# A transformer block on one core: the turn from attention to the feed-forward layer is put in another order, and w_down is loaded one block per step

## The chip, the core and the metric

The kernel runs on one core of one Trainium2 chip. The metric is device time in microseconds (us) of that core. Engines are named as in the profile: PE is the tensor engine (PEld its weight loads), DVE the vector engine, ACT the scalar engine, POOL the GpSimd engine, SP the engine that issues every DMA of this kernel.

## The reference

One block on 1024 tokens of width 1024, in float32. The mixer's three branches (a convolution branch, a chunked mLSTM, and a differential attention with four heads) are joined and multiplied by `w_out`; then a residual with a layer norm, a feed-forward layer of width 4096 with a squared ReLU, and a second residual with a layer norm:

```python
mix = jnp.concatenate([y_conv, y_ml, y_da], axis=-1) @ w_out
x1  = layer_norm(ALPHA * x + mix, ln1_g, ln1_b)
h   = jnp.square(jax.nn.relu(x1 @ w_up))
out = layer_norm(ALPHA * x1 + h @ w_down, ln2_g, ln2_b)
```

## The kernel before, in words

**Precision.** Every float32 operand is split into a high and a low part (`split`: ACT casts to `hi` at L147, DVE subtracts to `lo` at L148), and each product is three matmuls: hi by hi, lo by hi, hi by lo.

**Order of the work.** Instructions carry a priority and a scheduler lists them by it when the program is built: `lane(k)` gives the priority k million, and a lower number goes first when both could go. What stands on an engine is then a fixed row, which the engine works off in order. SP is such a row too: a DMA that waits there holds up all DMAs behind it. Buffers are 47 slots of 128 x 1056 in four rings (X, W, T, G), joined to one ring F for the feed-forward part; a buffer's load waits on SP until the slot's last user is done.

**Out projection** (`out_proj`, L854): y (the joined branches, kept in DRAM as `ydram0` to `ydram7`) times `w_out`, in two calls. The first takes y's blocks 0 to 4, the second blocks 5 to 7 (the attention's), for eight rows of 128 tokens each: 18 matmuls of 128x512 per row, which DVE adds to `acc` (L895), then a norm per row (`stats` on DVE, L903 on ACT). A row of y is read back by three DMAs (`yraw`), cast (`yh`) and subtracted (`yl`). The attention's last head (`attention(3, ...)`, lane 2) stands between the calls: scores `s`, softmax (`pp`), transposes into `t`, `wth`/`wtl`, their product with the values into `t`, a square sum (`sqs`), and `yda`, which goes out to `ydram` in four stores of 256 tokens.

**The turn.** `x1_half(t4)` transposes four rows of `acc` on PE (32 transposes) into two tiles of `xr`; half 0 gives B11 and B21, half 1 gives B12 and B22.

**The feed-forward layer** is a Strassen-Winograd product: seven products P1, P2, P6, P5, P7, P3, P4 in that order instead of eight. P1 needs B11 of x1, P2 needs B21, P6 needs T2, P5 needs T1, P7 needs T3, P3 needs B22, P4 needs T4, where T1 = B12 - B11, T2 = B22 - T1, T3 = B22 - B12, T4 = B21 - T2 (`x1_combine`). P1 and P2 of a pair thus need the first token half alone. w_up is worked off in 16 pairs of blocks; `up(s, p)` is one product of pair s, 12 matmuls of 128x512, and after P4 `hidden(s)` squares and stores the pair's hidden blocks (`h`). w_down follows in 56 steps of 24 matmuls (two halves of the output, seven products, four blocks each); step n needs its hidden operand (`hraw`, read from `h`), and its block or a sum of blocks of w_down (B11, B21, T2, ...), all split; `down_prep` issues that three steps ahead. Before, all of w_down's B12, B22 and B21 of the first half are asked for at step 0, the rows of the residual (`acc_load`) right behind it.

## Time and profile before

| | |
|---|---|
| median of 3 runs | 1198.04 us (1197.0 to 1199.02) |
| profiled execution | 1196.94 us, span 1195.2 us |
| mean granted PE clock | 0.984 |
| busy PE, DVE, ACT | 1139.2, 840.5, 563.2 us |
| DMA | 179.86 MB, mean 150 GB/s |

Times in the rows below are us from the start of the span of this one execution. The 1.74 us between the span and its time lie outside the rows. A row of a timeline is one instruction or several merged (x32): start, duration, engine, line, operation, what it writes and reads, and in brackets how long the engine stood idle just before it and which instruction released it.

### The profile page before, as it was taken

Reading aid. Unit: us, or ns where it says so; the run is one execution under the profiler, and the core shown is the slowest. Engines: PE = TensorE matmul, PEld = TensorE weight load, DVE = VectorE, ACT = ScalarE, POOL = GpSimd, SP = SyncE. Lnnn points to the kernel's source line nnn. Section 1 sums busy time; section 2 is a strip of 40 time slices with the busy share of each in tenths; the row PEclk is TensorE's granted clock in tenths of the full one; section 3 lists DMA queues with packets and bytes.
Section 4 is the critical chain, followed back from the end, with each engine's and each line's share of the span. In section 5 each row is a group of like instructions: output and inputs, shape, how many; then the busy total and the mean of one; then the engine's idle time right before and its main releaser. Section 6 shows DMA issues by size and latency. Waiting matters only on the chain.

```text
span 1195.2 us, 14972 instructions
## 1 busy us (share of the span) xinstructions
PE 1139.2 (95%) x5630; PEld 934.5 (78%) x5630; DVE 840.5 (70%) x1255; ACT 563.2 (47%) x910; POOL 13.8 (1%) x12
## 2 busy tenths in 40 slices
PE   8999999999999999976999999999989999999993
PEld 6898778877897877764888888888868888888882
DVE  5999568864774648869666777655778576766758
ACT  5212473575764627466544454444625332345411
POOL 0000000000000000000000000000000000000013
PEclk9999999999999999987999999999999999999997
DMA  7202144436635662421556465543984544353303
GB/s 276 70 10 71 37 130 132 149 128 182 167 107 191 198 187 64 156 98 53 184 179 245 167 229 194 178 162 119 321 312 158 194 162 161 107 169 124 106 27 114
DMA packets 82648, 179.86 MB, mean 150 GB/s; under 512 B 7760, under 2 KB 29328, under 8 KB 82576
## 3 DMA queue, kind: packets, MB, share of 16 engines
q1 hardware_dynamic: 82576, 178.91, 45.0%
q8 instruction: 44, 0.72, 0.2%
q14 instruction: 28, 0.23, 0.1%
HBM read 120.12 MB, written 58.72 MB: 150 GB/s over the span
## 4 chain that ended last, share of the span: by engine, by line
PE 84%; DVE 7%; ACT 4%; DMA 3%; issue 2%; SPq 0%; DVEq 0%; ACTq 0%
PE f L933 49%; PE mm L112 25%; PE s L112 5%; PE t L112 3%; PE t L115 2%; DVE lo L148 1%; ACT pp L736 1%; DMA hraw<-h 1%; DMA raw<-in_w_out 1%; ACT xr L975 1%; DVE bst L798 1%; ACT pp L741 1%; DMA kh<-qk 1%; DVE nm L734 1%; DVE pp L742 1%
## 5 line engine op out<-in xcount | busy, mean ns | idle before, releaser
L933 PE MATMUL f<-hi 128*128 128x512 f32 x832 | 330.6, 397 | 22.4 <-ACT hi L147 22.4
L933 PE MATMUL f<-lo,hi 128*128 128x512 f32 x832 | 329.6, 396 | 0.5 <-DVE lo L148 0.5
L933 PE MATMUL f<-hi,lo 128*128 128x512 f32 x832 | 328.4, 395 | 0.9 <-DVE lo L148 0.8
L933 PEld LDWEIGHTS f<-hi 128*128 128x128 f32 x832 | 158.2, 190 | 60.0 <-ACT hi L147 24.2
L933 PEld LDWEIGHTS f<-hi,lo 128*128 128x128 f32 x832 | 157.3, 189 | 38.8 <-DVE lo L148 2.8
L933 PEld LDWEIGHTS f<-lo,hi 128*128 128x128 f32 x832 | 158.2, 190 | 36.7 <-DVE lo L148 1.0
L147 ACT CAST hi<-hraw 128x1024 fp32r<-128x1024 f32 x56 | 58.1, 1048 | 104.7 <-DMA hraw<-h 93.2
L148 DVE TENSOR_TENSOR lo<-hraw,hi 128x1024 fp32r<-128x1024 f32 x56 | 68.3, 1222 | 51.1 <-ACT hi L147 48.5
L112 PE MATMUL mm<-xh,hi 128*128 128x512 f32 x240 | 95.8, 400 | 5.6 <-ACT xh L147 5.6
L112 PE MATMUL mm<-xl,hi 128*128 128x512 f32 x240 | 95.9, 400 | 0.0
L112 PE MATMUL mm<-xh,lo 128*128 128x512 f32 x240 | 95.9, 400 | 0.0
L285 DVE SCALAR_TENSOR_TENSOR cacc<-ypad,pc,cacc 128x1024 f32<-128x1024 f32 x60 | 74.2, 1278 | 0.6
L112 PE MATMUL mm<-hi,xh 128*128 128x256 f32 (+1 forms) x256 | 74.0, 289 | 0.0
L112 PE MATMUL mm<-hi,xl 128*128 128x256 f32 (+1 forms) x256 | 73.2, 286 | 0.0
L112 PE MATMUL mm<-lo,xh 128*128 128x256 f32 (+1 forms) x256 | 73.1, 286 | 0.0
L736 ACT ACTIVATE pp<-s,nm 128x128 f32<-128x128 f32 (+7 forms) x64 | 47.7, 747 | 28.7 <-DVE nm L734 19.7
L734 DVE TENSOR_REDUCE nm<-s 128x1 f32<-128x128 f32 (+7 forms) x64 | 47.9, 751 | 17.0 <-PE s L112 16.6
L147 ACT CAST hi<-B 128x1024 fp32r<-128x1024 f32 x32 | 33.5, 1050 | 50.6 <-PE f L933 34.5
L112 PEld LDWEIGHTS mm<-xh,hi 128*128 128x128 f32 x240 | 45.6, 190 | 14.3 <-ACT xh L147 5.6
L148 DVE TENSOR_TENSOR lo<-raw,hi 128x1024 fp32r<-128x1024 f32 (+3 forms) x34 | 39.2, 1160 | 24.2 <-ACT hi L147 19.8
L112 PE MATMUL mm<-hi,yh 128*128 128x512 f32 x128 | 50.9, 399 | 2.9 <-DVE tl L148 1.7
L112 PEld LDWEIGHTS mm<-xl,hi 128*128 128x128 f32 x240 | 45.6, 190 | 9.2 <-DVE xl L148 0.4
(258 smaller groups left out, 2039.1 us busy)
## 6 DMA issues: line engine op xcount, KB each, us to landing
hraw<-h SPq DMA_DIRECT2D x56, 512.0 KB, 3.5
w<-in_w_up SPq DMA_DIRECT2D x32, 512.0 KB, 3.9
B<-in_w_down SPq DMA_DIRECT2D x32, 512.0 KB, 5.9
h<-hp SPq DMA_DIRECT2D x16, 512.0 KB
h<-hq SPq DMA_DIRECT2D x16, 512.0 KB, 2.8
h<-hx SPq DMA_DIRECT2D x16, 512.0 KB, 4.4
raw<-in_wfm SPq DMA_DIRECT2D x14, 512.0 KB, 3.4
qk<-th SPq DMA_DIRECT2D x8, 512.0 KB
```

The lines of the kernel that those rows point to most:

```text
L112: return nc.tensor.matmul(out, lhsT=lhsT, rhs=rhs, start=start, stop=stop)
L115: nc.tensor.transpose(out, in_, ident[:k, :k])
L147: act.copy(hi, src)
L148: dve.tensor_tensor(out=lo, in0=src, in1=hi.bitcast(F32), op=ALU.subtract)
L285: dve.scalar_tensor_tensor(out=av, in0=yp[:, i:i + S], scalar=col(PC_DWW + 31 * c + i), in1=av, op0=ALU.mult, op1=ALU.add)
L734: dve.tensor_reduce(out=nm[:, m:m + 1], in_=s_[:, 0:nk], axis=AX.X, op=ALU.max, negate=True)
L736: act.activation(pp[m][:, 0:nk], s_[:, 0:nk], AF.Exp, bias=nm[:, m:m + 1], accum_out=sm[:, m:m + 1])
L741: act.activation(pp[1][:, 0:nk], pp[1][:, 0:nk], AF.Copy, scale=sm[:, 1:2])
L742: dve.scalar_tensor_tensor(out=pp[0][:, 0:nk], in0=pp[0][:, 0:nk], scalar=sm[:, 0:1], in1=pp[1][:, 0:nk], op0=ALU.mult, op1=ALU.add)
L798: dve.bn_stats(out=st[:, i, :], in_=z[:, i * (D // n):(i + 1) * (D // n)])
L933: return nc.tensor.matmul(out, lhsT=lhsT, rhs=rhs, start=start and not more, stop=stop and not more, skip_group_check=more)
L975: act.activation(xraw[kb // 4, t4][kb % 4 // 2][:, css[kb % 2]], t_, AF.Identity, scale=col(PC_L1G + kb), bias=col(PC_L1B + kb))
```

## The change

The attention's last head is emitted after a new lane 5, which holds the splits of `w_out`'s blocks 5 to 7 and the loads, sums and first splits of w_up's pairs 0 and 1. Rings X and W are joined to F before the last head, G after it, and the second `out_proj` takes all its buffers from F. `out_proj` calls `after_row` behind each row: it stores the row (`zdram`), loads pair 2 of w_up behind row 0, and behind row 5 emits `x1_half(0)` with its splits. `x1_half` now fills two banks at a time, and ACT and DVE evacuate one each. `x1_combine` is cut into five parts, and P1 and P2 of pairs 1 and 2 come before the first P6; then pairs 0 and 1 are worked off in turns. In the down part the blocks of w_down are loaded one or two per step, B11 and B21 from the last two up pairs on; the sums follow one per step, and for the first half T4 is written over B21.

```diff
-    def out_proj(kbs, first, rings, yring):
+    def out_proj(kbs, first, rings, yring, after=None):
...
                     act.activation(z, z, AF.Identity, scale=mv[:, 2:3], bias=mv[:, 4:5])
+                    after(tb)
         for r, w in zip(rings, wo):
             r.free(*w)
         early.clear()
 
     out_proj([0, 1, 2, 3, 4], True, [W] * NEARLY + [X] * (5 - NEARLY), lambda tb: X)
     X.give(W.take(2 * NEARLY))
-    with lane(2):
-        attention(3, neglam, dag)
-    out_proj([5, 6, 7], False, [X, G, G], lambda tb: X if tb > 1 else G)
-    psA.close()
-    ps_f = ctx.enter_context(tc.tile_pool(name="ps_f", bufs=1, space=bass.MemoryType.PSUM,
-                                          reuse_waits="tile"))
 
     F = Slots(spool, [])
-    for ring in (X, W, T, G):
+
+    def adopt(ring):
         F.q.extend(ring.q)
         F.of.update(ring.of)
+        ring.q.clear()
+
+    adopt(X)
+    adopt(W)
     zdram = [dram.tile([P, D], F32, name=f"z{i}") for i in range(TB)]
...
@@ -965,35 +965,52 @@
 
     xraw, xq = {}, {}
 
-    def x1_half(t4):
-        for kb in range(KB):
-            if kb % 4 == 0:
-                xraw[kb // 4, t4] = [F.alloc(F32, "xr") for _ in range(2)]
-            t_ = bank()
-            for j in range(4):
-                tr(t_[:, j * P:j * P + P], acc[4 * t4 + j][:, kb * P:kb * P + P])
-            act.activation(xraw[kb // 4, t4][kb % 4 // 2][:, css[kb % 2]], t_, AF.Identity,
-                           scale=col(PC_L1G + kb), bias=col(PC_L1B + kb))
+    def x1_half(t4, two_banks):
+
+        for i in range(2):
+            xraw[i, t4] = [F.alloc(F32, "xr") for _ in range(2)]
+        for kb in (0, 4, 2, 6):
+            t_ = two_banks()
+            for k in range(2):
+                for j in range(4):
+                    tr(t_[k][:, j * P:j * P + P],
+                       acc[4 * t4 + j][:, (kb + k) * P:(kb + k) * P + P])
+                o = xraw[kb // 4, t4][kb % 4 // 2][:, css[k]]
+                g_, b_ = col(PC_L1G + kb + k), col(PC_L1B + kb + k)
+                if k == 0:
+                    act.activation(o, t_[k], AF.Identity, scale=g_, bias=b_)
+                else:
+                    dve.tensor_scalar(out=o, in0=t_[k], scalar1=g_, scalar2=b_, op0=ALU.mult,
+                                      op1=ALU.add)
 
...
         xq[name] = [halves_of(t, keep) for t in raw]
 
-    def x1_combine():
+    def x1_combine(part):
         b11, b21, b12, b22 = (xraw[k] for k in ((0, 0), (1, 0), (0, 1), (1, 1)))
-        t1, t2 = [F.alloc(F32, "t1") for _ in range(2)], [F.alloc(F32, "t2") for _ in range(2)]
         n = slice(0, 1024)
-        for j in range(2):
-            sub(t1[j][:, n], b12[j][:, n], b11[j][:, n])
-            sub(t2[j][:, n], b22[j][:, n], t1[j][:, n])
-        x1_split_later = [("T1", t1), ("T3", b12), ("B22", b22), ("T4", b21)]
-        for j in range(2):
-            sub(b12[j][:, n], b22[j][:, n], b12[j][:, n])
-            sub(b21[j][:, n], b21[j][:, n], t2[j][:, n])
-        F.free(*b11)
-        x1_split("T2", t2)
-        for name, raw in x1_split_later:
-            x1_split(name, raw)
+        if part == "T2":
+            t1, t2 = ([F.alloc(F32, m) for _ in range(2)] for m in ("t1", "t2"))
+            xraw["T1"], xraw["T2"] = t1, t2
+            for j in range(2):
+                sub(t1[j][:, n], b12[j][:, n], b11[j][:, n])
+                sub(t2[j][:, n], b22[j][:, n], t1[j][:, n])
+            F.free(*b11)
+            x1_split("T2", t2, True)
+        elif part == "T1":
+            x1_split("T1", xraw["T1"])
+        elif part == "T3":
+            for j in range(2):
+                sub(b12[j][:, n], b22[j][:, n], b12[j][:, n])
+            x1_split("T3", b12)
...
 
     def w_done(s, p):
         F.free(*wt[s].get(p + "t", ()))
+
+    with lane(5):
+        early += [load_split(F, a["w_out"][kb], D, False) for kb in (5, 6, 7)]
+        w_load(0)
+        w_sums(0)
+        w_split(0, "w1")
+        w_load(1)
+        w_sums(1)
+        w_split(1, "w1")
+    with lane(2):
+        attention(3, neglam, dag)
+    adopt(G)
+
+    def two_banks():
+        t_ = ps_s.tile([P, 1024], F32, name="s")
+        return t_[:, 0:512], t_[:, 512:1024]
+
+    def after_row(tb):
+        load(zdram[tb], acc[tb][:, :D])
+        if tb == 0:
+            w_load(2)
+        if tb == 5:
+            x1_half(0, two_banks)
+            x1_split("B11", xraw[0, 0], True)
+            x1_split("B21", xraw[1, 0], True)
+            F.free(*acc[0:4])
+
+    out_proj([5, 6, 7], False, [F] * 3, lambda tb: F, after_row)
+    psA.close()
+    ps_f = ctx.enter_context(tc.tile_pool(name="ps_f", bufs=1, space=bass.MemoryType.PSUM,
+                                          reuse_waits="tile"))
 
...
         def w(nme):
             return wd[c, g, nme][:, n]
 
-        if part == 0:
+        if part == "T1":
             wd[c, g, "T1"] = F.alloc(F32, "T1")
             sub(w("T1"), w("B12"), w("B11"))
+        elif part == "T2":
             wd[c, g, "T2"] = F.alloc(F32, "T2")
             sub(w("T2"), w("B22"), w("T1"))
-        else:
+        elif part == "T3":
             sub(w("B12"), w("B22"), w("B12"))
             wd[c, g, "T3"] = wd.pop((c, g, "B12"))
+        elif c == 0:
+            sub(w("B21"), w("B21"), w("T2"))
...
@@ -1220,68 +1276,79 @@
 
 
     with lane(6):
-        for tb in range(TB):
-            load(zdram[tb], acc[tb][:, :D])
-        w_load(0)
-        w_sums(0)
-        w_split(0, "w1")
-        w_load(1)
-    with lane(7):
-        x1_half(0)
-        x1_split("B11", xraw[0, 0], True)
-        x1_split("B21", xraw[1, 0], True)
-        F.free(*acc[0:4])
+        w_split(0, "x")
+        w_split(2, "w1", True)
     tc.cur_priority = 8000000
     up(0, "P1")
     up(0, "P2")
-    x1_half(1)
+    x1_half(1, lambda: (bank(), bank()))
     F.free(*acc[4:8])
-    w_sums(1)
-    w_split(1, "w1")
+    x1_combine("T2")
     up(1, "P1")
     up(1, "P2")
-    x1_combine()
-    w_split(0, "x")
+    x1_combine("T1")
     w_split(0, "y")
+    up(2, "P1")
+    up(2, "P2")
+    up(0, "P6")
+    w_split(1, "x")
+    up(0, "P5")
+    x1_combine("T3")
+    up(1, "P6")
     w_split(0, "w2")
+    up(1, "P5")
+    x1_combine("B22")
...
+    x1_combine("T4")
+    up(0, "P3")
+    w_split(1, "y")
+    up(0, "P4")
+    hidden(0)
...
-                elif p == "P3":
-                    w_split(1, "y")
-                elif p == "P4":
-                    w_split(1, "w2")
...
+            w_load(n + 1)
+        if n < NS:
+            if p == "P6" and s > 2:
+                w_sums(n)
+            elif p == "P5" and s > 2:
+                w_split(n, "w1")
+            elif p == "P7":
+                w_split(n, "x")
+            elif p == "P3":
+                w_split(n, "y")
+            elif p == "P4":
+                w_split(n, "w2")
+        if p == ("P6" if s == 2 else "P1"):
             hidden(s - 1)
         if 3 <= s < 3 + TB and p == "P2":
             residual(s - 3)
+        if s == NS - 2 and p in ("P7", "P3"):
+            wd_load(0, ("P7", "P3").index(p), ("B11",))
         if s == NS - 1:
             F.free(*(t for pair in xq[BOF[p]] for t in pair))
             k = ORDER.index(p)
-            if 1 <= k < 1 + GC:
-                wd_load(0, k - 1, ("B11",))
+            if k < 2:
+                wd_load(0, 2 + k, ("B11",))
+            elif k < 6:
+                wd_load(0, k - 2, ("B21",))
+            if k >= 3:
+                acc_load((k - 3,))
             if k >= 7 - AHEAD:
                 down_prep(k - (7 - AHEAD))
     hidden(NS - 1)
...
         k = n % (7 * GC)
         final = c == 1 and p == "P4"
-        if c == 0 and k == 0:
-            for q in range(GC):
-                wd_load(0, q, ("B12", "B22"))
-                wd_load(0, q, ("B21",))
+        if c == 0 and k < GC:
+            wd_load(0, k, ("B12",))
+        if c == 0 and 2 <= k < 2 + GC:
+            wd_load(0, k - 2, ("B22",))
         if n + AHEAD < NSTEP:
             down_prep(n + AHEAD)
         if g == 0:
...
                 gather(abank[tb], 4 + tb, 0)
                 last_norm(4 + tb)
-        if c == 0 and k == 0:
-            acc_load(range(4))
         if g == GC - 1 and not final:
...
         if c == 0:
-            if k < GC:
-                wd_sums(0, k, 0)
-            elif k < 2 * GC:
-                wd_sums(0, k - GC, 1)
-                F.free(wd.pop((0, k - GC, "B11")))
-            elif k == 2 * GC:
-                for q in range(GC):
-                    F.free(wd.pop((0, q, "B21")))
-                acc_load(range(4, 8))
+            if 1 <= k < 1 + GC:
+                wd_sums(0, k - 1, "T1")
+                F.free(wd.pop((0, k - 1, "B11")))
+            if GC <= k < 2 * GC:
+                wd_sums(0, k - GC, "T2")
+                wd_sums(0, k - GC, "T4")
+            elif 2 * GC <= k < 3 * GC:
```

On PE, at the end of the last head: `t_...<-cst,pp` are transposes of softmax weights, `t_...<-wth/wtl` the product with the values, `t_...<-sqs` the square sum, `mm_4434` belongs to the first out projection, `mm_4865`, `mm_4876`, `mm_4908` (before) and `mm_4917` (after) to rows 0 and 1 of the second. Before:

```order
L112 MATMUL mm_4434<-hi_4091,yl_4378 128x512
L112 MATMUL mm_4865<-hi_4841,yh_4835 128x512
...
L112 MATMUL mm_4876<-hi_4853,yh_4835 128x512
L115 MATMUL t_4778<-cst_67,pp_4754 128x128 x4
L115 MATMUL t_4785<-cst_67,pp_4754 128x128 x4
L112 MATMUL mm_4865<-lo_4854,yh_4835 128x512
...
L112 MATMUL t_4792<-wth_4713,vh_4022 128x256
...
L112 MATMUL mm_4908<-hi_4841,yh_4861 128x512
...
L112 MATMUL t_4792<-sqs_4818,onesr_70 128x256
L112 MATMUL mm_4908<-hi_4853,yh_4861 128x512
```

After:

```order
L115 MATMUL t_4818<-cst_67,pp_4787 128x128 x3
L115 MATMUL t_4848<-cst_67,pp_4824 128x128 x4
L112 MATMUL mm_4434<-hi_4091,yl_4378 128x512
L115 MATMUL t_4855<-cst_67,pp_4824 128x128 x4
L112 MATMUL t_4862<-wth_4783,vh_4022 128x256
...
L112 MATMUL t_4862<-sqs_4888,onesr_70 128x256 x2
L112 MATMUL mm_4917<-hi_4477,yh_4905 128x512
```

No matmul of the second out projection stands among the last head's any more: its row 0 comes behind the head's last square sum.

On SP, at the same place: `yda` are the last head's stores, `yraw` reads of y by row (`yraw_4831` is row 0 before, `yraw_4901` row 0 after; `yraw_5072`, `yraw_5115` and `yraw_5133` belong to later rows). Before:

```order
L118 DMA yraw_4831<-ydram5_81 128x128
L118 DMA yraw_4831<-ydram6_82 128x128
L118 DMA yraw_4831<-ydram7_83 128x128
...
L118 DMA ydram7_83<-yda_4828 128x256
L118 DMA yraw_5072<-ydram7_83 128x128
L118 DMA yraw_5115<-ydram7_83 128x128
```

After:

```order
L118 DMA w2_4508<-in_w_up 128x1024
L118 DMA w2_4954<-in_w_up 128x1024
L118 DMA ydram7_83<-yda_4898 128x256
L118 DMA yraw_5133<-ydram7_83 128x128
L118 DMA yraw_4901<-ydram5_81 128x128
L118 DMA yraw_4901<-ydram6_82 128x128
L118 DMA yraw_4901<-ydram7_83 128x128
L118 DMA z0_4451<-acc_4075 128x1024
```

Row 0's three reads moved from well ahead of the last head's last store to behind it, and behind a read of row 5's y that needs this store. Their slot is the one that held w1 of w_up's pair 1.

On SP, where the down part begins (`B11` to `B22` are blocks of w_down, `hraw` the hidden operand of a step, `h7<-h...` the four stores of a pair's hidden blocks; the last four such stores are those of pair 15). Before:

```order
L118 DMA B21_7661<-in_w_down 128x2x512
L118 DMA B12_7663<-in_w_down 128x2x512
L118 DMA B22_7665<-in_w_down 128x2x512
L118 DMA B21_7667<-in_w_down 128x2x512
L118 DMA hraw_7669<-h3_5218 128x1024
L118 DMA acc_7707<-r0_5207 128x1024
L118 DMA acc_7709<-r1_5208 128x1024
L118 DMA acc_7711<-r2_5209 128x1024
L118 DMA acc_7713<-r3_5210 128x1024
L118 DMA hraw_7719<-h0_5215 128x1024
```

After:

```order
L118 DMA acc_7631<-r3_4462 128x1024
L118 DMA hraw_7633<-h2_4469 128x1024
L118 DMA h7_4474<-hp_7496 128x2x512
L118 DMA h7_4474<-hq_7542 128x2x512
L118 DMA h7_4474<-hx_7643 128x2x512
L118 DMA h7_4474<-hy_7644 128x512
L118 DMA B12_7657<-in_w_down 128x2x512
L118 DMA hraw_7659<-h3_4470 128x1024
L118 DMA B12_7697<-in_w_down 128x2x512
L118 DMA hraw_7699<-h0_4467 128x1024
```

Behind pair 15's stores one block of w_down now stands ahead of step 3's `hraw` and one ahead of step 4's; before, four blocks stood ahead of the first and four rows of the residual between the two.

## Rows read from the trace of the kernel before

**Rows 1.** The page: busy time of each engine, and the chain that ended last
```profile
PE 1139.2 (95%) x5630; PEld 934.5 (78%) x5630; DVE 840.5 (70%) x1255; ACT 563.2 (47%) x910; POOL 13.8 (1%) x12
PE 84%; DVE 7%; ACT 4%; DMA 3%; issue 2%; SPq 0%; DVEq 0%; ACTq 0%
```

**Rows 2.** Windows: stretch, length, busy PE, PEld, DVE, ACT, POOL; clock, DMA share, GB/s
```profile
490.00:520.00 30.00, 29.94 (x146) 24.59 (x144) 28.66 (x84) 15.98 (x29) 0.00 (x0) 1.00 0.50 181
520.00:550.00 30.00, 17.41 (x80) 13.98 (x80) 19.14 (x23) 24.07 (x31) 0.00 (x0) 0.87 0.09 35
550.00:580.00 30.00, 24.22 (x89) 18.62 (x90) 22.65 (x26) 14.67 (x21) 0.00 (x0) 0.79 0.29 96
580.00:850.00 270.00, 270.00 (x1171) 219.89 (x1171) 177.78 (x225) 133.48 (x169) 0.00 (x0) 1.00 0.55 194
850.00:900.00 50.00, 44.67 (x186) 35.28 (x186) 38.18 (x38) 18.86 (x20) 0.00 (x0) 0.97 0.80 294
```

**Rows 3.** Timeline of PE at the turn
```profile
516.29 3.65 PE L115 MATMUL f<-cst,acc 128*128 128x128 f32 x32
526.42 0.79 PE L933 MATMUL f<-hi 128*128 128x512 f32 x1 [6.48 <-ACT hi L147]
...
535.09 3.65 PE L115 MATMUL f<-cst,acc 128*128 128x128 f32 x32
...
552.19 0.80 PE L933 MATMUL f<-hi 128*128 128x512 f32 x1 [7.89 <-ACT hi L147]
...
557.60 0.79 PE L933 MATMUL f<-hi 128*128 128x512 f32 x1 [3.33 <-ACT hi L147]
...
562.65 0.44 PE L933 MATMUL f<-hi,lo 128*128 128x512 f32 x1
...
574.25 0.40 PE L933 MATMUL f<-hi,lo 128*128 128x512 f32 x1
```

**Rows 4.** Timeline of DVE at the turn
```profile
537.20 2.56 DVE L950 TENSOR_TENSOR t<-xr 128x1024 f32<-128x1024 f32 x2 [1.16 <-ACT xr L975]
...
547.30 4.62 DVE L148 TENSOR_TENSOR lo<-t,hi 128x1024 fp32r<-128x1024 f32 x4
551.85 6.89 DVE L148 TENSOR_TENSOR lo<-xr,hi 128x1024 fp32r<-128x1024 f32 x6
```

**Rows 5.** Timeline of PE over the last head and row 0
```profile
482.73 0.50 PE L112 MATMUL mm<-lo,yh 128*128 128x512 f32 x1 [1.32 <-DVE lo L148]
...
495.99 0.39 PE L112 MATMUL mm<-hi,yh 128*128 128x512 f32 x1
```

**Rows 6.** Timeline of ACT: the last softmax step, and the last step before `yda`
```profile
473.26 1.11 ACT L736 ACTIVATE pp<-s,nm 128x1024 f32<-128x1024 f32 x1
...
489.58 0.42 ACT L779 ACTIVATE rs<-rs 128x256 f32<-128x256 f32 x1
```

**Rows 7.** The DMA queue's own timeline: the last store of `yda`, the read behind it
```profile
490.57 0.32 SPq L118 DMA_DIRECT2D ydram<-yda  x1
492.32 0.80 SPq L118 DMA_DIRECT2D yraw<-ydram  x2
```

**Rows 8.** DMA issues: count, KB each, median us from issue to landing
```profile
hraw<-h SPq DMA_DIRECT2D x56, 512.0 KB, 3.5
yraw<-ydram SPq DMA_DIRECT2D x64, 64.0 KB, 2.3
```

**Rows 9.** Timeline of PE where the down part begins
```profile
880.03 0.71 PE L933 MATMUL f<-hi 128*128 128x512 f32 x1 [4.67 <-ACT hi L147]
...
883.16 0.58 PE L933 MATMUL f<-hi 128*128 128x512 f32 x1
...
889.56 0.96 PE L933 MATMUL f<-hi,lo 128*128 128x512 f32 x3 [0.53 <-DVE lo L148]
```

**Rows 10.** The DMA queue's own timeline there
```profile
874.30 25.28 SPq L118 DMA_DIRECT2D hraw<-h  x8
```

**Rows 11.** Timeline of ACT there
```profile
878.93 1.04 ACT L147 CAST hi<-hraw 128x1024 fp32r<-128x1024 f32 x1 [5.08 <-DMA hraw<-h]
```

More of the change, by code (lines that the diff above doesn't have):

```diff
@@ L978, in x1_split @@
     def x1_split(name, raw, keep=False):
         xq[name] = [halves_of(t, keep) for t in raw]
-    def x1_combine():
+    def x1_combine(part):
         b11, b21, b12, b22 = (xraw[k] for k in ((0, 0), (1, 0), (0, 1), (1, 1)))
-        t1, t2 = [F.alloc(F32, "t1") for _ in range(2)], [F.alloc(F32, "t2") for _ in range(2)]
         n = slice(0, 1024)
-        for j in range(2):
-            sub(t1[j][:, n], b12[j][:, n], b11[j][:, n])
-            sub(t2[j][:, n], b22[j][:, n], t1[j][:, n])
-        x1_split_later = [("T1", t1), ("T3", b12), ("B22", b22), ("T4", b21)]
-        for j in range(2):
-            sub(b12[j][:, n], b22[j][:, n], b12[j][:, n])
-            sub(b21[j][:, n], b21[j][:, n], t2[j][:, n])
-        F.free(*b11)
-        x1_split("T2", t2)
-        for name, raw in x1_split_later:
-            x1_split(name, raw)
+        if part == "T2":
[12 more added lines that the diff above has]
+            x1_split("T3", b12)
+        elif part == "B22":
+            x1_split("B22", b22)
+        else:
+            for j in range(2):
+                sub(b21[j][:, n], b21[j][:, n], xraw["T2"][j][:, n])
+            F.free(*xraw["T2"])
+            x1_split("T4", b21)
@@ L1015, in w_sums, with w_split @@
         w.update(x=x, y=y)
-    def w_split(s, key):
+        if w["kept"]:
+            F.free(w1)
+    def w_split(s, key, keep=False):
         w = wt[s]
@@ L1026, in w_split @@
             return
-        hi, lo = halves_of(raw)
+        hi, lo = halves_of(raw, keep)
+        w["kept"] = keep
         n0, n1 = dict(w1=("P1", "P2"), x=("P5", "P6"), y=("P7", "P3"))[key]
@@ L1236, in mixer_block @@
     up(0, "P2")
-    x1_half(1)
+    x1_half(1, lambda: (bank(), bank()))
     F.free(*acc[4:8])
-    w_sums(1)
-    w_split(1, "w1")
+    x1_combine("T2")
     up(1, "P1")
     up(1, "P2")
-    x1_combine()
-    w_split(0, "x")
+    x1_combine("T1")
     w_split(0, "y")
-    w_split(0, "w2")
+    up(2, "P1")
[5 more added lines that the diff above has]
+    up(1, "P6")
+    w_split(0, "w2")
+    up(1, "P5")
+    x1_combine("B22")
+    up(0, "P7")
+    x1_combine("T4")
[3 more added lines that the diff above has]
+    hidden(0)
+    w_split(1, "w2")
+    w_sums(2)
+    w_load(3)
+    up(1, "P7")
+    w_split(2, "x")
+    up(1, "P3")
+    w_split(2, "y")
+    up(1, "P4")
+    w_split(2, "w2")
+    w_sums(3)
+    w_split(3, "w1")
     AHEAD = 3
-    todo = [(0, p) for p in ORDER[2:]] + [(1, p) for p in ORDER[2:]]
-    todo += [(s, p) for s in range(2, NS) for p in ORDER]
-    preps = []
+    todo = [(2, p) for p in ORDER[2:]] + [(s, p) for s in range(3, NS) for p in ORDER]
     for s, p in todo:
@@ L1340, in mixer_block @@
                 q = (k - 4 * GC - 2) // 2
-                wd_sums(1, q, 0)
+                wd_sums(1, q, "T1")
+                wd_sums(1, q, "T2")
         elif k < GC:
-            wd_sums(1, k, 1)
+            wd_sums(1, k, "T3")
+            wd_sums(1, k, "T4")
         elif k == 2 * GC:
```

25 lines of the change are left out of this document (6 added, 19 removed).

## The prediction

> **What bounds the kernel now.** I read the page first: PE is busy for 1139.2 of 1195.2 us, and the chain that ended last runs through PE for 84% [rows 1]. Whatever does not move a wait of PE moves nothing, so the rest is a search for PE's idle time. The windows place it: 490 to 520 has next to none (29.94 of 30 busy), 520 to 550 has 12.59, 550 to 580 has 5.78, 580 to 850 none, and 850 to 900 has 5.33 [rows 2]. The first two of these losses are the turn, the last is the start of the down part. The change touches these two places, and one more, the end of the last attention head, where PE had work to fill in.
>
> **What the turn costs.** PE waits 6.48 us for B11's first split, 7.89 for T2's first and 3.33 for a split that stands behind T1's to T4's; the windows have 18.37 us idle in all (12.59 + 5.78) [rows 2, 3]. After each long wait the granted clock is low (means of 0.87 and 0.79 in these windows [rows 2]) and matmuls come at about half rate: 10 of them in the 5.05 us from 557.60, against 50 in the 11.60 us from 562.65 to 574.25, 0.232 each [rows 3]. One product is 12 matmuls, 2.79 us at that rate. At 574.25 nine products and four matmuls of a tenth are done, so nine were at 573.3. From the projection's end at 516.29 that is 57.0 us, for two times 3.65 of transposes and 9 x 2.79 of products, 32.4: the turn loses 24.6, of which 18.4 are waits and 6.2 the slow clock and small change. The cause stands on DVE: eight subtractions lie between 537.20 and 547.30, at 1.14 from one start to the next, and only then come T2's and T1's splits (4 in 4.62) and six more (6.89), without a break [rows 4].
>
> **What the change makes of the turn.** PE gets more to do before T2: P1 and P2 of three pairs need only the first token half. And T2's four subtractions and two splits, 6 x 1.14 = 6.9 us on DVE, come ahead of the others. The price is in the part before it.
>
> *Row 0 of the second out projection.* Before, PE filled the last head's waits with rows 0 and 1: the projection ends at 516.29, and from 495.99 on there are 87 of its 144 matmuls (20.30 us at 0.233), so 57 were done by 496 [rows 3, 5]. In the new order on PE none stands among the head's, and on SP row 0's reads stand behind the last store of `yda` and a read that needs its landing. I follow that chain on the old time axis. PE reaches the last softmax earlier: fifteen matmuls of rows 0 and 1 no longer stand ahead of the last transposes and the score block is earlier on PE, so the step at 473.26 comes at about 470.4 (an estimate). Before, the step ahead of `yda` began 16.3 us after it and the store was issued 17.3 after it [rows 6, 7]. If that held, the store goes at 487.7. But DVE's row now has sums of w_up (half as wide as the subtractions of [rows 4], so some 0.6 each) and splits of w_out (1.15 each, as the splits there) ahead of the square sum; with up to five us of these in the chain it goes at 493. I take 490.0, between the two: PE waited for DVE there even before (1.32 [rows 5]), so not all of that work finds cover. Then: 1.75 us until the next read leaves (490.57 to 492.32 [rows 7]), 0.4 for it and two reads of 0.4 before row 0's last one leaves at 492.95, 2.3 to land [rows 8], about 0.7 for cast and start: row 0 begins at 496.0. Bounds 493.7 and 499.
>
> The Trainium skill, DMA: Bandwidth & Descriptors, section on the anatomy of one DMA, gives every DMA a fixed cost of about 2.0 us, most of it the receipt of the last write, and bytes over 436 GB/s on top. By that the store (128 KB) would take 2.3 where the row shows 1.75, and the read (64 KB) 2.15 where the row shows 2.3: the sum would come out 0.4 us later. The rule speaks against the change, since it puts two such costs in a row ahead of PE's next work; the rows decide its size.
>
> So the projection is 57 matmuls behind: 57 x 0.233 = 13.2 us later than before, and the long idle time ahead of it makes some 12 matmuls slow, 2.4 more: it would end at 531.9. Half 0's 32 transposes (3.65 [rows 3]) now lie inside its last two rows: 535.6. What they hide is the evacuation and the split of B11 and B21, which cost the wait of 6.48 and its slow matmuls. The cover is thin: DVE is busy for 28.66 of 30 us under the projection [rows 2], and four evacuations and four splits are added at its end. By my count DVE has B21's last split at about 537.6, and P2 asks for it at 538.5. I cost this at nothing; if the cover fails, the four splits, 4 x 1.15 = 4.6, are the most.
>
> *From there.* P1 and P2 of pair 0 run to 541.2. Half 1's transposes wait for the norm of row 7. No row has that wait: from 516.29 to 526.42 norm, transposes, evacuation and first split took 10.1 us together [rows 3], so it is done by 545.7 at the latest, and the wait is 0 to 4.5; I take 1.7, as the norm is less than half of these steps plus DVE's backlog. Transposes 3.65, P1 and P2 of pairs 1 and 2 11.2: 557.7. T2 needs evacuations, subtractions and splits behind 546.5, about 9 us: 555.5, in time by 2. After that each product takes 2.79 and the operands come in the order T1, T3, B22, T4 with DVE some 2 to 4 us ahead of PE; no wait, and no slow matmul. Nine products are done at 557.7 + 3 x 2.79 = 566.1, against 573.3. **The turn gains 7.2 us**: 24.6 recovered, less 13.2 and 2.4 at row 0 and 1.7 at row 7. With the bounds of row 0 and row 7 alone it is between 4.4 less and 4.0 more gained than that; the four splits would take 4.6 of it.
>
> **The down part.** Step 0 waits 4.67 us, there is one more wait of 0.53, and 7 slow matmuls lie between 880.03 and 883.16, some 1.4: 6.6 us [rows 9]. It waits for an `hraw` whose cast had itself waited 5.08 for the DMA [rows 11]; later `hraw` are issued at 874.30, behind all the blocks of w_down and four rows of the residual on SP [rows 10]. After the change B11, B21 and the rows lie before the up part's end, the first three `hraw` ahead of pair 15's stores, and one 512 KB block ahead of the fourth. That one is wanted three steps of 5.6 us after the up part ends, 16.7; it stands on SP behind pair 15's stores, which wait for some eight steps of ACT and DVE of 0.6 to 1.1 each, so it leaves about 7.5 after it, lands in 3.5 [rows 8], and is cast (1.04 [rows 11]) and split (1.15 [rows 4]); with 1.6 of queue on DVE, 14.8. Step 1's split has about one us to spare. I take 6.3 gained, bounds 6.6 and 0. **The other moves** (row stores behind each row, the sums spread over steps, T4 over B21) I cost at nothing: from 580 to 850 PE never waits, with DVE busy for 177.78 of 270 us [rows 2], so there is room for a subtraction (1.14) that comes later; without that cover each would cost its 1.14.
>
> **Sum.** 1196.94 - 7.2 - 6.3 = 1183.4 us for an execution like the profiled one. The median of the three runs is 1.10 above that: 1184.5.
>
> **Rivals.**
> *Row 0 early.* The store goes at 487.7 and DVE keeps up: row 0 begins at 493.7 (2.3), no wait for row 7's norm comes (1.7), and the clock is not lost (2.4): 1178. For it: DVE had idle time in the head's tail, as one third of its time overall [rows 1]. Against: PE's row is fixed and in order, so nothing of row 0 can pass the head; to have back the 13.2 would need another order. Chance 0.14.
> *The gain goes elsewhere.* Either DVE falls behind under rows 6 and 7 (4.6) and row 0 begins at 499 (3), or `hraw` stays late, since w_down's bytes are the same and only their place changed (6.3): about 1191. For it: DVE's 28.66 of 30 and the one us of margin at step 1. Against: the loads now start some 25 us before they are wanted. Chance 0.23.
> *Slower.* The one mechanism that could do it is the head of line on SP ahead of row 0: its reads wait for a store, for the slot of w_up's pair 1, and so for that pair's load, sums and split on DVE. Every us there is a us of PE. It makes the kernel slower by over 0.2% once row 0 begins 16 us later than I say, at 512 (13.5 of gain and 2.4). For it: no row shows what DVE's row costs there. Against: a load (some 4 us, as `hraw`'s 3.5 [rows 8]), four sums (2.4) and a split on both engines (2.3) add up to 9. Time some 1203. Chance 0.07.
> *It doesn't do what it says.* That T2 is waited for behind three pairs as long as before would need DVE some 18 us behind; its work there is the same as before. It is in the second rival's chance.
>
> **Chances and range.** The forecast, 1180 to 1188, has 0.50. Row 0 early (1174 to 1180) 0.14, the gain elsewhere 0.23 (1188 to 1195.6), no change 0.06, slower 0.07. A measurement tells 0.2% from no change, 2.4 us: faster below 1195.6. So faster 0.87, same 0.06, slower 0.07. The range 1175 to 1195 leaves out the last two and the ends of the first two rivals, some 0.18.
>
> **What would show it.** In the new profile: a wait of PE of 8 to 12 us ahead of row 0's first `mm<-hi,yh`, released by ACT's `yh`, and a low clock behind it; no wait over 1 us between P1 and P2 of pair 0 and none for T2; at most 3 us ahead of the transposes of half 1; no wait at the down part's start. If the wait ahead of row 0 is under 5 us or over 15, the chain on SP and DVE was mis-sized; if T2 is still waited for, the count of DVE's work was.

## The result, and the profile after

| | before | after |
|---|---|---|
| median, us (4 runs each, on one chip) | 1198.53 (1197.0 to 1202.15) | 1182.53 (1181.23 to 1185.73) |
| profiled execution, its span | 1196.94, 1195.2 | 1181.23, 1179.4 |
| mean granted PE clock | 0.984 | 0.986 |

The ratio is 0.9866 (0.9835 to 0.9897): 16.0 us or 1.3% faster. 1184.5 was forecast, 1175 to 1195 as the range.

The page after, busy times and the shares of the chain of waits:

```profile
PE 1135.5 (96%) x5630; PEld 932.5 (79%) x5630; DVE 848.3 (72%) x1263; ACT 558.8 (47%) x902; POOL 13.8 (1%) x12
...
PE 88%; DVE 6%; DMA 2%; ACT 2%; issue 1%; SPq 0%; DVEq 0%; ACTq 0%
```

The bound is the same engine with the same work; 88% of the chain stands on it where 84% did [rows 1]. The windows say where its idle time went (span of time and its length, then busy time of PE, PEld, DVE, ACT and POOL with instruction counts, granted clock, DMA share, GB/s):

```profile
460.00:490.00 30.00, 20.98 (x117) 15.96 (x116) 26.89 (x44) 21.12 (x41) 0.00 (x0) 0.90 0.59 189
490.00:520.00 30.00, 25.07 (x96) 20.25 (x97) 18.96 (x50) 8.58 (x16) 0.00 (x0) 0.82 0.19 70
520.00:550.00 30.00, 29.07 (x159) 23.78 (x158) 27.96 (x56) 23.01 (x33) 0.00 (x0) 1.00 0.22 89
550.00:580.00 30.00, 30.00 (x132) 24.44 (x131) 28.98 (x33) 19.50 (x25) 0.00 (x0) 1.00 0.12 42
580.00:850.00 270.00, 270.00 (x1169) 219.40 (x1168) 178.53 (x228) 134.75 (x170) 0.00 (x0) 1.00 0.59 209
850.00:900.00 50.00, 50.00 (x218) 40.70 (x217) 44.13 (x44) 23.12 (x25) 0.00 (x0) 1.00 0.74 275
```

Against [rows 2], the idle 12.59 and 5.78 us of the turn are 0.93 and 0, the 5.33 of the down part's start are 0, and the low clock has moved from 520 to 580 into 460 to 520. There 4.93 us are idle from 490 to 520, and 9.02 from 460 to 490, where the kernel before had 2.80:

```profile
460.00:490.00 30.00, 27.20 (x150) 21.77 (x150) 24.23 (x40) 20.02 (x42) 0.00 (x0) 1.00 0.33 96
```

So the change does not only take waits away, it brings one forward into the end of the attention head. The list of PE's waits (total, times, longest) names it, with PE's timeline at the same places:

```profile
PE mm L112 <- ACT yh L147: 9.2, 1, 9.2
...
PE f L115 <- ACT acc L903: 0.9, 2, 0.6
```

```profile
484.53 1.18 PE L112 MATMUL t<-sqs,onesr 128*128 128x256 f32 x2 [2.35 <-ACT sqs L147]
494.93 0.80 PE L112 MATMUL mm<-hi,yh 128*128 128x512 f32 x1 [9.21 <-ACT yh L147]
495.52 0.63 PE L112 MATMUL mm<-lo,yh 128*128 128x512 f32 x1
...
501.06 0.42 PE L112 MATMUL mm<-hi,yl 128*128 128x512 f32 x1
...
534.95 0.39 PE L933 MATMUL f<-hi 128*128 128x512 f32 x1
...
541.45 0.76 PE L115 MATMUL f<-cst,acc 128*128 128x128 f32 x5 [0.56 <-ACT acc L903]
542.58 2.95 PE L115 MATMUL f<-cst,acc 128*128 128x128 f32 x25 [0.37 <-ACT acc L903]
545.28 0.47 PE L933 MATMUL f<-hi 128*128 128x512 f32 x1
```

Row 0 of the out projection begins at 494.93 behind a wait of 9.21 us and runs its first fourteen matmuls at about half rate (6.13 us for the fourteen steps from 494.93 to 501.06, 0.44 each, where [rows 3] have 0.232; that is 2.9 us more than at the full rate). P1 of pair 0 begins at 534.95 without a wait, half 1's transposes wait 0.93 in all, and from 545 to 1130 PE waits for nothing.

**Two stretches.** Executions differ by up to 5 us in what lies ahead of the turn (a store of `yda` that all kernels have leaves SP between 433.2 and 437.9 in the profiled ones), so I compare stretches of one trace as well. The last product of the up part stands at 858.39 before and 850.35 after; from there to the span's end it is 336.81 and 329.05. From that store, at 433.24 before and 433.64 after, to that last product it is 425.15 and 416.71. So the turn gave 8.4 us (8.0 on the span's axis; 7.2 was forecast) and the down part 7.8 (6.3 was forecast).

### The profile page after: what moved, and what is told of

Same layout as the page of the kernel before. It is cut to its first block, busy times and chain, and to the rows that moved or that the text cites. A ratio compares the mean times of both kernels' runs of the same rounds, so it can differ in the third digit from the quotient of the medians.

```text
span 1179.4 us, 14960 instructions
## 1 busy us (share of the span) xinstructions
PE 1135.5 (96%) x5630; PEld 932.5 (79%) x5630; DVE 848.3 (72%) x1263; ACT 558.8 (47%) x902; POOL 13.8 (1%) x12
## 4 chain that ended last, share of the span: by engine, by line
PE 88%; DVE 6%; DMA 2%; ACT 2%; issue 1%; SPq 0%; DVEq 0%; ACTq 0%
PE f L933 50%; PE mm L112 27%; PE s L112 5%; PE t L112 4%; PE t L115 2%; DMA raw<-in_w_out 1%; DVE bst L798 1%; DVE lo L148 1%; ACT pp L736 1%; DMA vh<-v 0%; DVE bmv L807 0%; DVE nm L734 0%; DVE acc L953 0%; DMA v<-vh 0%; DVE acc L1266 0%
## 5 line engine op out<-in xcount | busy, mean ns | idle before, releaser
L933 PE MATMUL f<-hi 128*128 128x512 f32 x832 | 327.1, 393 | 0.0
L147 ACT CAST hi<-B 128x1024 fp32r<-128x1024 f32 x36 | 37.6, 1049 | 52.0 <-PE f L933 39.3
L148 DVE TENSOR_TENSOR lo<-B,hi 128x1024 fp32r<-128x1024 f32 x36 | 43.8, 1221 | 18.7 <-ACT hi L147 13.1
```

Source lines behind the costliest of these rows:

```text
L147: act.copy(hi, src)
L148: dve.tensor_tensor(out=lo, in0=src, in1=hi.bitcast(F32), op=ALU.subtract)
L933: return nc.tensor.matmul(out, lhsT=lhsT, rhs=rhs, start=start and not more, stop=stop and not more, skip_group_check=more)
```

## The experiments

Medians are us; "stretch" is that from the store of `yda` near 435 to the last up product, in the profiled execution. Ratios are to the kernel before as it was measured again beside each group of runs, with their 95% interval; its medians there were 1198.44 (e1 to e4), 1199.38 (e5 to e8) and 1199.03 (e9, e10), so a difference of medians between groups carries up to 1 us. A stretch is one execution: e1, whose turn is that of the kernel before, differs from it by 1.35.

| kernel | median | ratio | stretch |
|---|---|---|---|
| before | 1198.53 | 1 | 425.15 |
| changed | 1182.53 | 0.9866 (0.9835 to 0.9897) | 416.71 |
| e1, down part alone | 1191.51 | 0.9941 (0.9926 to 0.9956) | 423.80 |
| e2, turn alone | 1192.80 | 0.9948 (0.9935 to 0.9962) | 416.78 |
| e3, row 0 early | 1172.56 | 0.9779 (0.9767 to 0.9792) | 407.18 |
| e4, two pairs | 1183.57 | 0.9873 (0.9858 to 0.9887) | 416.76 |
| e5, sums first, three pairs | 1188.82 | 0.9912 (0.9899 to 0.9926) | 423.61 |
| e6, sums first, two pairs | 1194.53 | 0.9956 (0.9942 to 0.9969) | 426.64 |
| e7, filled wait | 1181.24 | 0.9850 (0.9837 to 0.9864) | 413.66 |
| e8, row 0 early and lighter | 1170.71 | 0.9762 (0.9749 to 0.9776) | 404.74 |
| e9, half 0 behind | 1186.28 | 0.9892 (0.9875 to 0.9910) | 421.08 |
| e10, no early w_out splits | 1178.51 | 0.9826 (0.9810 to 0.9843) | 411.47 |

### Which part gives what (e1, e2)

e1 is the kernel before with the down part's new order alone:

```diff
+        if s == NS - 2 and p in ("P7", "P3"):
+            wd_load(0, ("P7", "P3").index(p), ("B11",))
...
-        if c == 0 and k == 0:
-            for q in range(GC):
-                wd_load(0, q, ("B12", "B22"))
-                wd_load(0, q, ("B21",))
+        if c == 0 and k < GC:
+            wd_load(0, k, ("B12",))
+        if c == 0 and 2 <= k < 2 + GC:
+            wd_load(0, k - 2, ("B22",))
```

> The kernel before with the down part's change alone (w_down's blocks one or two per step, sums one per step, T4 over B21, rows of the residual early); the turn is as before. Theory (the two gains are separate, and the down part's is the wait for a hidden operand behind w_down's blocks on SP): PE no longer waits at the down part's start, 6.3 to 7.8 us faster than before, a ratio of 0.9935 to 0.9948, and the turn's waits of 6.48, 7.89 and 3.33 are all there. Rival (the gain comes with the turn, since an earlier up part moves the loads too): within 2 us of before.

e2 is the changed kernel with the old down part, the same lines the other way round:

> The changed kernel with the down part as before. Theory: the turn gains 7 to 8 us, ratio 0.993 to 0.994; the wait of about 9 us ahead of row 0 is there, none for T2, and the down part's start again waits 4 to 5 us for the split of a hidden operand. With the run of the down part alone the two gains add up to that of the whole change, 15 to 16 us. Rival: they overlap, so the sum of the two is several us more or less than the whole.

The timeline of PE in e1, and then in e2:

```profile
528.26 0.80 PE L933 MATMUL f<-hi 128*128 128x512 f32 x1 [6.47 <-ACT hi L147]
...
553.48 0.80 PE L933 MATMUL f<-hi 128*128 128x512 f32 x1 [7.88 <-ACT hi L147]
558.88 0.80 PE L933 MATMUL f<-hi 128*128 128x512 f32 x1 [3.33 <-ACT hi L147]
```

```profile
873.41 0.79 PE L933 MATMUL f<-hi 128*128 128x512 f32 x1 [4.96 <-ACT hi L147]
883.22 0.96 PE L933 MATMUL f<-hi,lo 128*128 128x512 f32 x3 [0.53 <-DVE lo L148]
```

e1 keeps the three waits of the turn as in [rows 3] and has none at the down part's start; e2 keeps the two of the down part as in [rows 9] and has none in the turn. From the last up product to the span's end e1 takes 329.13, as the changed kernel's 329.05, and e2 337.21, as the 336.81 before. The two gains in the traces, 8.4 of e2's stretch and 7.7 of e1's down part, add up to 16.1, where the whole has 16.2. By medians they are 6.9 and 5.6 and add up to 12.5, less than the 15 to 16 that I expected; the product of the ratios, 0.9889, lies within the interval of the whole. The traces thus show two separate gains, and the medians do not speak against it.

### What row 0's place costs (e3, e7, e10, e8)

e3 gives rows 0 and 1 buffers of ring G again, so that their reads no longer stand behind the last head's store on SP:

```diff
-    adopt(G)
...
+        if tb < 2:
+            adopt(G)
...
-    out_proj([5, 6, 7], False, [F] * 3, lambda tb: F, after_row)
+    out_proj([5, 6, 7], False, [F] * 3, lambda tb: F if tb > 1 else G, after_row)
```

> The changed kernel, but rows 0 and 1 of the second out projection take their buffers from the ring G, which is joined to F only behind each of these rows; their reads of y then leave SP ahead of the last head's last store. Theory (the wait ahead of row 0 is the order on SP, and its price is matmuls not done plus the slow clock): the wait of 9.2 us shrinks to under 2, PE works on rows 0 and 1 from about 485 on, and the kernel is 9 to 15 us faster than the changed one, 1168 to 1174. Rival (DVE bounds the projection, with w_up's sums and splits in its row): most of the gain is given back as waits for DVE under the rows, 1177 to 1182.

PE's timeline of e3, and its windows from 490 to 550:

```profile
484.12 0.50 PE L112 MATMUL mm<-hi,yh 128*128 128x512 f32 x1 [0.71 <-ACT hi L147]
...
524.48 1.42 PE L115 MATMUL s<-cst,acc 128*128 128x128 f32 x8 [1.71 <-ACT xr L981]
525.56 0.77 PE L933 MATMUL f<-hi 128*128 128x512 f32 x1
...
528.26 0.97 PE L933 MATMUL f<-hi 128*128 128x512 f32 x2
```

```profile
490.00:520.00 30.00, 28.56 (x129) 22.57 (x127) 29.25 (x73) 11.49 (x21) 0.00 (x0) 1.00 0.26 98
520.00:550.00 30.00, 27.54 (x136) 22.32 (x136) 25.89 (x44) 24.04 (x34) 0.00 (x0) 0.94 0.18 74
```

The wait of 9.21 is gone, and the kernel is 10.0 us faster than the changed one by medians, 9.5 by the stretch. PE's idle time accounts for it: over the stretch PE is idle for 14.98 us in the changed kernel (416.71 less 401.73 busy) and for 5.74 in e3 (407.18 less 401.44), 9.2 less. The largest parts are, in the changed kernel, 9.21, the 2.35 for `sqs` and 1.78 for `wtl` ahead of it, and 0.93 at half 1; in e3 1.07 in three short waits around row 0 and 3.76 in five waits of 0.20 to 1.71 at half 0's transposes. Slow matmuls are on both sides, 2.9 us in the changed kernel and 1.3 in e3 (2.70 us for the six steps from 525.56 to 528.26, with a clock of 0.94 in that window). DVE is now busy for 29.25 of 30 us under the projection and the transposes wait for the evacuation. So both sides of the expectation showed: the head of line was worth most of it, and some 5 us were given back.

e7 adds 24 throwaway matmuls into a bank that row 0 then overwrites, ahead of row 0, and leaves nothing out:

```diff
+                    for _ in range(24 if not first and tb == 0 and nh == 0 else 0):
+                        wl = wt[1]["P1"][1]
+                        mm(ps, wl[:, 0:P], wl, True, True)
```

> The changed kernel with 24 matmuls of 128x512 more on PE ahead of row 0's first, in the wait of 9.2 us; their operand is a low part of w_up that is ready some 2 us into the wait, and their sum is thrown away, since row 0's first matmul overwrites it. Theory (the price of the wait is the time that PE stands plus some 2.3 us of slow clock behind it): row 0 still begins at about 495, its first 12 matmuls come at 0.23 instead of 0.43, and the kernel is 2 us faster, 1180 to 1181, with more work done. Rival (the slow matmuls behind the wait cost nothing, since DVE sets the pace of the rows): within 0.7 us of the changed kernel.

```profile
489.81 7.56 PE L112 MATMUL mm<-lo 128*128 128x512 f32 x24 [1.42 <-DVE lo L148]
497.67 0.50 PE L112 MATMUL mm<-hi,yh 128*128 128x512 f32 x1 [0.30 <-ACT yh L147]
498.01 0.39 PE L112 MATMUL mm<-lo,yh 128*128 128x512 f32 x1
```

In this timeline of e7 row 0 still waits for `yh`, but runs at full rate from its second matmul on. The stretch is 3.0 us shorter, which is what the changed kernel's slow matmuls cost by their rows (2.9). By medians it is 1.3, with intervals that overlap; the medians alone would not show it. The traces say why they can differ: in e7's profiled execution the store of `yda` ahead of the turn left 3.0 us later (436.64 for 433.64), which hides the gain in its time.

e10 leaves the early splits of w_out's last blocks out of lane 5 and is otherwise the changed kernel:

```diff
-        early += [load_split(F, a["w_out"][kb], D, False) for kb in (5, 6, 7)]
```

> The changed kernel without the early splits of w_out's blocks 5 to 7: the second out projection loads and splits them itself. The buffers then fall in another order, and on SP row 0's reads of y stand ahead of the last head's last two stores again, while one block of w_out stands just ahead of the last store. Theory (the wait ahead of row 0 comes from the order of buffers, in which the early blocks of w_out pushed row 0's reads to the slot of w_up's pair 1): row 0 starts inside the head, and the wait for the last block of w_out that takes its place is shorter, 3 to 6 us; 2 to 7 us faster than the changed kernel, 1176 to 1181. Rival (w_out's late block makes PE wait as long as y did): row 0 can't go on before about 493, 1181 to 1184.

The first two rows are PE's timeline of e10, the third one is SP's, the fourth ACT's:

```profile
482.23 0.50 PE L112 MATMUL mm<-hi,yh 128*128 128x512 f32 x1 [0.51 <-ACT yh L147]
...
492.27 1.22 PE L112 MATMUL mm<-hi,yh 128*128 128x512 f32 x2 [7.55 <-ACT hi L147]
```

```profile
486.65 0.33 SPq L118 DMA_DIRECT2D raw<-in_w_out  x1
```

```profile
491.17 1.04 ACT L147 CAST hi<-raw 128x1024 fp32r<-128x1024 f32 x1 [3.92 <-DMA raw<-in_w_out]
```

Row 0's reads move ahead of the last stores by themselves, because three fewer buffers are taken from ring F before them; row 0 begins at 482.23. It then waits 7.55 for the last block of w_out, whose load leaves at 486.65. I had expected 3 to 6 there, and that size was off; even so it is 4.0 us faster than the changed kernel by medians, with intervals that touch, and 5.2 by the stretch. Splitting w_out early thus cost this kernel time, and for the most part by the buffer slots, which set the order on SP: from the store of `yda` near 435 to the last one it is 53.88 us in e10 and 55.27 in the changed kernel, so at most 1.4 of the 5.2 is the work that left the head.

e8 is e3 with two pairs begun instead of three, and with the splits of pair 0's sum and of pair 2 moved behind the projection:

```diff
-    with lane(6):
-        w_split(0, "x")
-        w_split(2, "w1", True)
...
     x1_combine("T2")
+    w_split(0, "x")
...
-    up(2, "P1")
-    up(2, "P2")
     up(0, "P6")
     w_split(1, "x")
+    w_split(2, "w1", True)
```

> Rows 0 and 1 from ring G as in the run that has row 0 early, two pairs begun, and the splits of w_up's pair 0 (sum) and pair 2 moved from under the projection to behind it, which takes 2.4 us off DVE where it is busy for 29.25 of 30. Theory (there DVE now sets the pace: 4 us of waits at half 0's transposes come from row 3's late norm): 2 to 3 us faster than row 0 early, 1169 to 1171. Rival (the two banks of the transposes set the pace, not DVE): no change, 1172 to 1173.

1170.71 (1169.14 to 1172.82, 5 runs) is the fastest of all here, faster than both kernels. Its gain over e3, 1.9 by medians (2.4 by the stretch), is within the overlap of the intervals; two things were changed at once, so which of them gave it is not shown. PE's waits at half 0's transposes and behind them:

```profile
523.75 1.32 PE L115 MATMUL s<-cst,acc 128*128 128x128 f32 x8 [0.55 <-ACT xr L981]
525.35 0.49 PE L933 MATMUL f<-hi 128*128 128x512 f32 x1 [0.28 <-ACT hi L147]
526.30 0.50 PE L933 MATMUL f<-hi 128*128 128x512 f32 x1 [0.46 <-ACT hi L147]
```

They sum to 1.29 where e3's five had 3.76; half 1's transposes, which waited for nothing in e3, wait 1.14, and the product behind them another 0.28. The clock stays at 1.00 from 520 to 550, so e3's 1.3 us of slow matmuls are gone too. Part of the crowding is gone, and part has moved on by one step.

### What covers T2 (e4, e5, e6)

e4 puts P1 and P2 of the third pair back behind the first two pairs:

```diff
-    up(2, "P1")
-    up(2, "P2")
     up(0, "P6")
...
-    todo = [(2, p) for p in ORDER[2:]] + [(s, p) for s in range(3, NS) for p in ORDER]
+    todo = [(s, p) for s in range(2, NS) for p in ORDER]
```

> The changed kernel with two pairs begun on the first token half, as before: P1 and P2 of pair 2 come behind pair 1's P4. T2's splits are then wanted 5.6 us earlier. Theory (the third pair is what covers T2, with 2 to 3.5 us to spare): PE waits 2 to 4 us for T2 and T1 and loses some clock, 1185 to 1188. Rival (bringing T2 ahead on DVE was enough, the third pair does nothing): 1182 to 1183.

My theory fell: nothing waits for T2, and the stretch is 416.76 against 416.71. A new theory was needed: that it is the order of the sums and splits, T2's and T1's ahead of the others, that took the waits away. I call it DVE's order; the splits' casts on ACT move along with it. e5 keeps three pairs and puts the old order of sums back (all eight, then all ten splits); e6 does so with two pairs:

```diff
-    x1_combine("T2")
+    x1_combine()
     up(1, "P1")
     up(1, "P2")
-    x1_combine("T1")
...
-    x1_combine("T3")
...
-    x1_combine("B22")
...
-    x1_combine("T4")
```

> The changed kernel with three pairs begun, but with x1's sums as before the change: all eight subtractions first, then the ten splits, T2's first. With the run of two pairs, which showed no wait for T2, two theories are left. Theory A (DVE's order is what removed the turn's two waits, the third pair is spare): T2's splits come 4 to 5 us later than in the changed kernel, which the third pair's 5.6 us cover, so no wait or one under 1 us, 1182 to 1184. Theory B (the order of DVE matters beyond T2, since T1's and the other splits and w_up's stand behind): PE waits 2 to 4 us in the products that follow, 1185 to 1188.

> The same old order of x1's sums, with two pairs begun, as before. Theory A: neither cover is there, and the waits ahead of the first P6 come back, 6 to 11 us with the slow clock behind them: 1189 to 1195, about the turn's gain lost. Rival (what removed the waits is that half 1's evacuation is shared between ACT and DVE and the transposes start earlier): 1183 to 1185.

DVE's timeline of the changed kernel, then DVE's, ACT's and PE's of e5, then PE's of e6:

```profile
549.38 1.22 DVE L148 TENSOR_TENSOR lo<-t,hi 128x1024 fp32r<-128x1024 f32 x1
550.52 1.22 DVE L950 TENSOR_TENSOR t<-xr,t 128x1024 f32<-128x1024 f32 x1
551.65 1.22 DVE L148 TENSOR_TENSOR lo<-t,hi 128x1024 fp32r<-128x1024 f32 x1
552.79 0.68 DVE L953 TENSOR_TENSOR hp<-hp,f 128x512 f32<-128x512 f32 x1
553.39 2.36 DVE L148 TENSOR_TENSOR lo<-t,hi 128x1024 fp32r<-128x1024 f32 x2
```

```profile
554.87 4.63 DVE L148 TENSOR_TENSOR lo<-t,hi 128x1024 fp32r<-128x1024 f32 x4
559.41 6.90 DVE L148 TENSOR_TENSOR lo<-xr,hi 128x1024 fp32r<-128x1024 f32 x6
```

```profile
565.20 0.59 ACT L1098 COPY hp<-f 128x512 f32<-128x512 f32 x1 [1.22 <-DVE lo L148]
566.39 0.59 ACT L1103 COPY hq<-f 128x512 f32<-128x512 f32 x1 [0.60 <-DVE lo L148]
```

```profile
567.03 0.80 PE L933 MATMUL f<-hi 128*128 128x512 f32 x1 [3.87 <-ACT hq L1103]
```

```profile
558.23 0.80 PE L933 MATMUL f<-lo,hi 128*128 128x512 f32 x1 [4.80 <-DVE lo L148]
...
567.99 0.50 PE L933 MATMUL f<-hi 128*128 128x512 f32 x1 [2.32 <-ACT hq L1103]
```

In the changed kernel the first split of T1 or T2 starts at 549.38 and the fourth ends at 555.75; in e5 the four lie from 554.87 to 559.50 and are followed by six more without a break. With the old order, two pairs are not enough (4.80 and 2.32 of wait) and three still leave one wait: that of 3.87, released by ACT's copy of a product out of its bank (`hq`), which itself had stood in ACT's row behind copies that waited for DVE's splits (1.22 and 0.60). The four medians: new order 1182.5 with three pairs and 1183.6 with two, old order 1188.8 and 1194.5. By medians and by stretches DVE's order is worth 6 to 7 with three pairs and 10 to 11 with two; the third pair is worth 3 to 6 with the old order and about 1 or nothing with the new. The new order alone does nearly all of it. e6's rival, that the shared evacuation of half 1 had taken the waits away, fell: e6 has that evacuation and waits.

Why two suffice can be read in the order of e4's instructions on PE: behind one matmul of P6 the scheduler puts seven of P5, which start on the first half of T1 (its split is the first of the four on DVE), then mixes the two products, and draws four matmuls of pair 2's P1 in between. The operand that comes first is used first, whatever order the source begins the products in.

### What half 0's place is worth (e9)

```diff
-        if tb == 5:
-            x1_half(0, two_banks)
-            x1_split("B11", xraw[0, 0], True)
-            x1_split("B21", xraw[1, 0], True)
-            F.free(*acc[0:4])
...
+    with lane(7):
+        x1_half(0, two_banks)
+        x1_split("B11", xraw[0, 0], True)
+        x1_split("B21", xraw[1, 0], True)
+        F.free(*acc[0:4])
```

> The changed kernel, but half 0's 32 transposes and the splits of B11 and B21 stand behind the second out projection, as before, instead of inside its last rows. Theory (the rows hide the evacuation and the first split, which cost the wait of 6.48 us before): a wait of 4 to 6.5 us ahead of pair 0's P1 and slow matmuls behind it, 5 to 8 us slower than the changed kernel, 1187 to 1191. Rival (DVE sets the pace of this stretch, 28 of 30 us, so moving its work out from under the rows moves the end of the rows forward by as much): within 2 us of the changed kernel.

The largest of its six waits, in PE's timeline:

```profile
535.85 1.09 PE L115 MATMUL s<-cst,acc 128*128 128x128 f32 x8 [0.98 <-DVE bmv L804]
```

It is 3.8 us slower than the changed kernel by medians, with intervals that overlap, and 4.4 by the stretch, between the theory's 5 to 8 and the rival's 2. There is no single wait of 4 us or more and no low clock from 520 to 550 (1.00), but six waits of 0.15 to 0.98, 3.7 in all: with ACT and DVE each evacuating one bank, the transposes and the splits follow each other more closely than in [rows 3]. So hiding half 0 under the projection is worth some 4, not the 6.48 and the slow matmuls that I had counted as one lump. I put the rest down to the new evacuation; no run has it alone, so that is not shown.

## Why the prediction was right, and where it was not

- **Row 0.** Held, a us better: 494.93 for 496.0, bounds 493.7 and 499. The last softmax step came at 469.68 (470.4 was the estimate), `yda` was stored at 488.91 (490.0), and the next read left 1.76 later (1.75). From that step to the store it is 19.2 us, 1.9 more than the 17.3 before; up to five were allowed for DVE's new work. The 490.0 was taken between two bounds and not worked out, so its nearness is in part luck.

```profile
488.91 0.33 SPq L118 DMA_DIRECT2D ydram<-yda  x1
490.67 2.08 SPq L118 DMA_DIRECT2D yraw<-ydram  x4
```

  These two rows, the store and the reads behind it, are SP's timeline of the changed kernel. The wait, 9.21, is inside the forecast 8 to 12, is released by `yh`, and the slow matmuls behind it cost 2.9 (2.4), as fourteen and not twelve of them came slow. By the fit in the Trainium skill (DMA: Bandwidth & Descriptors, Anatomy of one DMA — SWDGE (gpsimd) path) the store would take 2.3 us, an estimate. The section gives this fit for DMAs that GpSimd issues, not for every DMA as I wrote, and here SP issues them; the two traces have 1.75 and 1.76 from the store's issue to that of the read that needs it, and the measurement decides.
- **Half 0's thin cover.** Held, thinner than forecast. B21's last split ends at 537.29 (537.6); P2 asks for it at 534.95 + 2.79 = 537.74, so 0.45 us were left where I had 0.9:

```profile
536.07 1.22 DVE L148 TENSOR_TENSOR lo<-xr,hi 128x1024 fp32r<-128x1024 f32 x1
```

- **Row 7's norm.** 0.93 for 1.7, within the bounds of 0 and 4.5; the term was mis-sized by 0.77. The turn's lower bound was added up wrongly: 3.0 at row 0 and 2.8 at row 7 are 5.8 less, not 4.4. Neither was reached.
- **"P1 and P2 of three pairs" as what covers T2.** This step failed, though its sum came out. T2's splits were in time, as forecast (the four end at 555.75 by the row above, P6 begins behind 545.28 + 4 x 2.79 = 556.4), but e4 shows that the third pair isn't what makes them so. DVE's order, which stood in the prediction as the second half of one step, is the larger half.
- **The turn.** 8.0 on the span's axis, on which the forecast was worked out (8.4 by the stretch), for 7.2. The terms explain it: 1.07 at row 0 and 0.77 at row 7 are 1.8 better than forecast, and the rest together 1.0 worse, half of it the two more slow matmuls at row 0 (2.9 for 2.4).
- **The down part.** The mechanism held (e1, e2): no `hraw` is waited for. The size did not: 7.8 is above my upper bound, 6.6. In part that is my own counting of [rows 9]: from 880.03 to 883.16 lie 3.13 us for six steps, which at 0.232 would be 1.39, so the slow matmuls cost 1.74 and not 1.4; 4.67 + 0.53 + 1.74 = 6.9. The windows say more: from 850 to 900 PE runs 186 matmuls before [rows 2] and 218 after, and 32 of them at 0.232 are 7.4 us. Only the 0.4 behind 900 stays open.
- **A label was wrong.** I wrote that step 0 waits 4.67 us. The down part's first matmul stands at 858.62, and three steps of 5.6 us run before 880.03: it is step 3 that waits, for the `hraw` that SP issued at 869.74 behind four blocks of w_down. The cause was as I put it, the step was not. Its cast waited for it until 878.93 [rows 11], 9.2 us after the issue, where the median to land is 3.5 [rows 8]. So not all of the delay was its place on SP; I take the rest to be the bytes of the blocks ahead of it (294 GB/s from 850 to 900 [rows 2]), which no run separates. After, SP's timeline has a block and an `hraw` in turn:

```profile
857.37 0.64 SPq L118 DMA_DIRECT2D hraw<-h  x1
858.11 0.43 SPq L118 DMA_DIRECT2D B<-in_w_down  x1
858.63 0.42 SPq L118 DMA_DIRECT2D hraw<-h  x1
```

- **The rivals.** The early row 0 did not come with this order, as argued, and e3 shows what it takes (another ring for its buffers) and that it is worth more than the forecast's 6 (10). The gain did not go elsewhere, and the head of line on SP did not reach the 16 us that would have decided it.

## What to carry to other kernels

Where a scheduler takes buffers from a ring, the slot decides where a load stands on the one queue that issues all DMAs: before anything is moved earlier, look at which reads will then stand behind a store that is late. When operands are late, first reorder the engine that makes them, so that the one needed first is finished first, and only then find other work to cover the rest; here the first was worth 6 to 11 us and the second, on top of it, about one or nothing. Measure two parts that were meant for one wait apart and together, since either may be enough.
